# Low products at the seam of two up-projection pieces, and down steps gathered between the pairs

## The chip, the cores and the metric

The kernel runs on one core of one Trainium2 chip. The metric is the device time of one execution in microseconds (us). Five engines work side by side, each through its own list of instructions in order: TensorE multiplies matrices (in the profile PE, and PEld for its loads of stationary operands), VectorE (DVE) and ScalarE (ACT) do elementwise work, GpSimd (POOL) and SyncE (SP) here mostly start DMA transfers. An instruction that waits for a semaphore holds up everything behind it on its own engine.

## The reference

One layer of a hybrid encoder on a sequence of 256 tokens with model width 2048. The part that matters here is the convolutional feed-forward block at its end; the mixer ahead of it uses one changed helper as well.

```
x  = x + hybrid_mixer(rms_norm(x, attn_norm), ...)      # two kinds of attention, 16 heads
h  = rms_norm(x, ffn_norm)
u  = h @ w_up                                           # 2048 -> 2 * 5632, float32
u  = causal depthwise conv of width 3 over u, + conv_b  # per feature
gate, val = split(u)
x  = x + (silu(gate) * val) @ w_down                    # 5632 -> 2048
```

All inputs and outputs are float32.

## The kernel before, in words

**Precision.** TensorE is fed with the rounded type fp32r. Every operand is therefore kept as two parts, a high part (the value rounded to fp32r) and a low part (what the rounding lost), and a product is made as high x high + high x low + low x high. A weight tile of 128 x 2048 numbers (1 MB) arrives by a DMA in `w_raw`; ACT copies it to `w_hi` (line 202), then DVE computes `w_lo = w_raw - w_hi` (line 203). This pair is called the split of a tile. In the feed-forward block there are three buffers each for `w_hi` and `w_lo` and four for `w_raw`.

**Up steps.** The 11264 columns of `w_up` are made 256 at a time. Such a result is called a pair here, because it is made in two pieces: piece a takes the first 1024 of the 2048 rows, piece b the rest, both into the same two PSUM banks `pu` (`from_features`, line 244). A piece has 16 products with `w_hi`, each with 512 moving columns (activation high and low parts side by side; called wide), and 16 products with `w_lo` with 256 moving columns (high part alone; called narrow). Before the change both pieces do the wide ones first and then the narrow ones. The same helper makes queries and keys of the second kind of heads in the mixer, by way of `feature_major` (line 263), with two buffers for `w_hi` and two for `w_lo` there.

**Down steps.** The feed-forward width of 44 blocks of 128 features is cut into six parts: five of 8 blocks and a last one of 4. A part of 8 blocks is multiplied with its rows of `w_down` by a scheme that saves one of eight block products (`down_in_seven`, line 946): 7 steps for each half of the 2048 output columns, so 14 steps, called s1 to s14 here (s8 to s14 are the second half). Each has 12 wide products into one PSUM bank and afterwards one DVE addition of this bank into `x` (`added`, line 941). The banks of s1 to s7 are a, b, c, a, a, b, a; s8 to s14 repeat this with new tiles. The weights of s2, s4 and s7 (and s9, s11, s14) are three successive contents of one tile `w_sum`: DVE forms it from two loaded tiles (line 994), s2 splits it, then GpSimd starts a DMA that adds a third tile onto it in memory (`plus`, line 964), s4 splits the new content, another such DMA adds onto it, and s7 splits that. Beside the first of these DMAs a second one adds onto the loaded tile that s5 (s12) will use. The `w_sum` pool has one buffer.

**The order of the work.** The down steps of a part run between the up steps of the next part. A string tells how: u is the next up piece, s the next down step; `ORDER` serves the first five parts (the first has no down steps to do), `LAST_ORDER` the last, where the digits stand for the plain down product of the last part itself. The up pairs of a part are called P1 to P8 here: gate, value, gate, value and so on.

The loop at line 1094 writes all engines' instructions in this order by hand. In its pass n it issues, in this order: the load of step n+6; one advance of all follow-up work; the split of step n+2 (and the adding DMAs that hang on it); a second advance; the sum at line 994 for step n+4; and the products of step n. Follow-up work is a generator per step, advanced twice in a pass: for a down step the addition into `x` comes in the pass after it, ahead of that pass's split. For a pair it begins in the pass after piece b: ACT copies half of the PSUM result (842) and DVE adds and scales (843, 845) behind that pass's split; ACT makes the convolution taps (852, 859) a pass later; DVE sums them (864, and 879 for a value) ahead of the split in the third pass, and for values an ACT copy and DVE work (882, 884, and in some pairs 896 to 899, 906, 911) follow in the fourth and fifth.

In the mixer the instructions are ordered by a planner instead.

Of the kernel before, what the change touches and what calls it, by code (L numbers as in the profile page):

```python
# [14 lines left out]
P = 128  # L15
D = 2048
S = 256
NT = S // P
KT = D // P
# [18 lines left out]
FFN_PARTS = [(f, min(f + 8, NFT)) for f in range(0, NFT, 8)]  # L38


ORDER = "uuusususususususususususususus"
LAST_ORDER = "uususususususussss0s1ss3s2"


@with_exitstack
def hybrid_layer(
# [19 lines left out]
    nc = tc.nc  # L66
# [65 lines left out]
    hT = big.tile([P, KT, 2, S], F32R, name="hT")  # L132
# [99 lines left out]
    def token_major(lhs, w, k0, nk, c0, cols):  # L232

        acc = psa.tile([P, NT, 512], F32, name="acc", tag="acc")
        for k in range(0, nk, 4):
            parts = weights(rows_of(w, k0 + k, 4, c0, cols), 4, cols)
            in_three(
                [acc[:, t, :cols] for t in range(NT)], parts, 4,
                lambda i, part, t: of_half(lhs(k + i), part, t), k == 0, k + 4 == nk,
            )  # L240
            step()
        return acc

    def from_features(acc, parts, kh, n=8):

        hi, lo = parts
        for i0 in range(0, 8, n):
            for i in range(i0, i0 + n):
                k = 8 * kh + i
                for j in range(2):  # L250
                    nc.tensor.matmul(  # L251
                        acc[:, j, :], hi[:, i, j * P : (j + 1) * P],
                        hT[:, k].rearrange("p a b -> p (a b)"), start=k == 0, stop=False,
                    )
            for i in range(i0, i0 + n):
                k = 8 * kh + i
                for j in range(2):
                    nc.tensor.matmul(  # L258
                        acc[:, j, S:], lo[:, i, j * P : (j + 1) * P], hT[:, k, 0, :],
                        start=False, stop=k == KT - 1,  # L260
                    )

    def feature_major(w, c0, pool, tag):

        acc = pool.tile([P, 2, 512], F32, name="pu", tag=tag)
        for kh in range(2):
            from_features(acc, weights(rows_of(w, 8 * kh, 8, c0, 2 * P), 8, 2 * P), kh)
            step()
        return acc
# [9 lines left out]
    with ExitStack() as actx:  # L279
# [9 lines left out]
        def project(c0, cols):  # L289
            return token_major(lambda k: hT[:, k], wi, 0, KT, c0, cols)  # L290
# [198 lines left out]
        low = big.tile([P, 2, 16 * P], F32R, name="low", tag="x2")  # L489
# [41 lines left out]
        for j in range(3):  # L531
            acc = project(2 * WF + 344 * j, 344)
            n = 344 if j < 2 else 336
# [212 lines left out]
        for half in range(2):  # L746
# [6 lines left out]
            acc = project(B0 + 2 * WF + 512 * half, 512)  # L753
# [16 lines left out]
        for group in range(2):  # L770
# [3 lines left out]
            for c in range(4):  # L774
                acc = token_major(lambda k: oT[group * NH + k], wo, group * NH, NH, 512 * c, 512)
# [6 lines left out]
                if c == 0:  # L782
                    pg = psb.tile([P, NT], F32, name="pg", tag="t")
                    for t in range(NT):
                        nc.tensor.matmul(
                            pg[:, t : t + 1], ssq[group][:, t * P : (t + 1) * P], ones[:, 0:1],
                            start=t == 0, stop=t == NT - 1,
# [125 lines left out]
    def up_pieces(part, f0, follows):  # L913

        c0 = f0 * P + (DFF if follows is val_follows else 0)
        cell = []

        def piece(kh):
            mem = {}

            def loads():
                mem["raw"] = load(rows_of(wu, 8 * kh, 8, c0, 2 * P))

            def prepare():
                mem["parts"] = split(mem["raw"], 8, 2 * P)

            def matmuls():
                if kh == 0:
                    cell.append(psa.tile([P, 2, 512], F32, name="pu", tag="acc"))
                from_features(cell[0], mem["parts"], kh, 8 if c0 else 4)  # L930

            new_step(loads, None, prepare, matmuls, (lambda: follows(part, cell[0], f0)) if kh else None)

        piece(0)
        yield
        piece(1)
        yield
# [76 lines left out]
    def down_plain(part, c):  # L1014

        n = (part.f_hi - part.f_lo) // 4

        ends = LAST_ORDER[-1] == str(c // 512)
        sizes = [(0, 0, 512), (1, 0, 256), (1, 256, 256)] if ends else [(t, 0, 512) for t in range(NT)]
# [45 lines left out]
    for f_lo, f_hi in FFN_PARTS:  # L1065
# [9 lines left out]
        if f_hi == NFT:  # L1075
            steps_of |= {str(i): [down_plain(part, 512 * i)] for i in range(4)}
        for g in ORDER if f_hi < NFT else LAST_ORDER:
            if steps_of[g]:
# [81 lines left out]
```

## Time and profile before

| what | value |
|---|---|
| median of 3 runs | 1105.21 us (1105.05 to 1105.63) |
| the profiled execution's own time | 1106.53 us |
| its span, first to last instruction | 1104.8 us |
| granted TensorE clock over the span | 1.00 |
| busy share of the span | PE 99%, PEld 86%, DVE 79%, ACT 64%, POOL 4% |
| up pieces (32 products each) | 104: 88 in the feed-forward block, 16 in the mixer |
| down steps of 12 products | 70 |

The times of the profile are in microseconds from the first instruction. A row of the timeline gives start, duration, engine, line, operation, tiles written and read with their shapes, and how many instructions were merged; brackets give idle time ahead of it and what ended that. Matmuls overlap, so the length of a run of products is read from its start to the start of the next run, not from its duration.

### The profile page before, as it was taken

The numbers are of one execution on the slowest core, as the hardware profiler recorded it, in microseconds if no ns is written. First come the engines' busy times: TensorE is split into PE (matmuls) and PEld (weight loads), VectorE is DVE, ScalarE is ACT, GpSimd is POOL, SyncE is SP. The second block draws the span as 40 slices with busy tenths as digits, with TensorE's granted clock in tenths as the row PEclk, the third lists the DMA queues.
The fourth block names the chain that finished last, engine by engine and source line by source line (L and its number), as shares of the span: only waits on it lengthen the run. The fifth ranks groups of instructions, "written<-read, shape, count | busy, mean of one in ns | idle before, by whom it ended". The sixth has DMA issues, their size and how long they took to land. (4 is left out here: it accounts for less than half of the span.)

```text
span 1104.8 us, 14832 instructions
## 1 busy us (share of the span) xinstructions
PE 1098.9 (99%) x5872; PEld 951.9 (86%) x5872; DVE 875.6 (79%) x940; ACT 701.9 (64%) x879; POOL 44.4 (4%) x46
## 2 busy tenths in 40 slices
PE   9999999999999999999999999999999999999998
PEld 7998888888888888888888888888888888888887
DVE  5755777677775677679889988889798889889896
ACT  6544555556653567667767776767676677667753
POOL 0000000000000000000000010100000010100010
PEclk9999999999999999999999999999999999999999
DMA  8776555557555395558989597986979688987985
GB/s 290 183 230 229 189 156 156 187 153 247 173 161 184 113 313 196 194 181 204 292 222 311 190 235 263 263 268 177 317 208 308 210 222 273 253 266 192 325 212 161
DMA packets 179407, 245.96 MB, mean 223 GB/s; under 512 B 4432, under 2 KB 119018, under 8 KB 179082
## 3 DMA queue, kind: packets, MB, share of 16 engines
q1 hardware_dynamic: 162458, 209.73, 58.2%
q0 software_dynamic: 16560, 34.75, 16.7%
q8 instruction: 46, 0.75, 0.3%
q10 hardware_dynamic: 320, 0.53, 0.1%
q14 instruction: 23, 0.19, 0.0%
HBM read 242.89 MB, written 2.11 MB: 222 GB/s over the span
## 5 line engine op out<-in xcount | busy, mean ns | idle before, releaser
L203 DVE TENSOR_TENSOR w_lo<-w_raw,w_hi 128x2048 fp32r<-128x2048 f32 (+1 forms) x196 | 439.7, 2246 | 148.4 <-ACT w_hi L202 147.7
L202 ACT CAST w_hi<-w_raw 128x2048 fp32r<-128x2048 f32 (+1 forms) x196 | 367.1, 1876 | 255.6 <-PE pu L251 77.8
L251 PE MATMUL pu<-hT,w_hi 128*128 128x512 f32 x1664 | 397.0, 390 | 0.0
L251 PEld LDWEIGHTS pu<-hT,w_hi 128*128 128x128 f32 x1664 | 309.4, 188 | 62.4
L258 PEld LDWEIGHTS pu<-hT,w_lo 128*128 128x128 f32 x1664 | 213.6, 191 | 8.2
L258 PE MATMUL pu<-hT,w_lo 128*128 128x256 f32 x1664 | 216.5, 283 | 0.0
L224 PE MATMUL acc<-w_hi,hT 128*128 128x512 f32 (+1 forms) x576 | 125.8, 369 | 0.0
L224 PEld LDWEIGHTS acc<-w_hi,hT 128*128 128x128 f32 x576 | 101.3, 188 | 14.1
L202 ACT CAST w_hi<-w_sum 128x2048 fp32r<-128x2048 f32 x30 | 57.3, 1910 | 43.3 <-PE pu L251 36.5
L203 DVE TENSOR_TENSOR w_lo<-w_sum,w_hi 128x2048 fp32r<-128x2048 f32 x30 | 68.7, 2289 | 19.9 <-ACT w_hi L202 19.8
L859 ACT ACTIVATE tap<-up,ccol 128x256 f32<-128x256 f32 x176 | 74.6, 495 | 0.0
L224 PE MATMUL acc<-w_lo,hT 128*128 128x512 f32 (+1 forms) x288 | 64.6, 366 | 0.0
L224 PEld LDWEIGHTS acc<-w_lo,hT 128*128 128x128 f32 x288 | 51.6, 188 | 7.5
L964 POOL DMA_DIRECT2D w_sum<-in_w_down_dram x20 | 25.7, 1285 | 769.8 <-DVE w_lo L203 758.5
L224 PE MATMUL acc<-w_hi,oT 128*128 128x512 f32 x192 | 46.2, 393 | 0.0
L224 PEld LDWEIGHTS acc<-w_hi,oT 128*128 128x128 f32 x192 | 35.6, 188 | 7.3
L224 PE MATMUL bank_a<-w_hi,s 128*128 128x512 f32 x160 | 40.1, 393 | 0.8 <-ACT w_hi L202 0.8
L224 PE MATMUL bank_a<-w_hi,g 128*128 128x512 f32 x160 | 40.0, 392 | 0.0
L224 PE MATMUL bank_b<-w_hi,s 128*128 128x512 f32 x160 | 40.0, 392 | 0.0
L224 PEld LDWEIGHTS bank_a<-w_hi,s 128*128 128x128 f32 x160 | 28.8, 189 | 6.4 <-ACT w_hi L202 1.2
L224 PEld LDWEIGHTS bank_a<-w_hi,g 128*128 128x128 f32 x160 | 28.9, 189 | 5.2
L224 PEld LDWEIGHTS bank_b<-w_hi,s 128*128 128x128 f32 x160 | 28.9, 189 | 5.3
(214 smaller groups left out, 1072.3 us busy)
## 6 DMA issues: line engine op xcount, KB each, us to landing
w_raw<-in_w_up_dram SPq DMA_DIRECT2D x88, 1024.0 KB, 7.6
w_raw<-in_w_down_dram SPq DMA_DIRECT2D x44, 1024.0 KB, 6.4
w_raw<-in_w_in_dram SPq DMA_DIRECT2D x36, 1024.0 KB, 5.2
w_sum<-in_w_down_dram POOLq DMA_DIRECT2D x20, 1024.0 KB, 10.1
w_raw<-in_w_out_dram SPq DMA_DIRECT2D x16, 1024.0 KB, 5.1
w_raw<-in_w_down_dram POOLq DMA_DIRECT2D x10, 1024.0 KB, 14.8
w_raw<-in_w_in_dram SPq DMA_DIRECT2D x12, 688.0 KB, 4.2
w_raw<-in_w_in_dram SPq DMA_DIRECT2D x6, 512.0 KB, 6.7
```

The lines of the kernel that those rows point to most:

```text
L202: act.copy(hi[:, :n], raw[:, :n])
L203: dve.tensor_tensor(lo[:, :n], raw[:, :n], f32(hi[:, :n]), op=ALU.subtract)
L224: nc.tensor.matmul(o, lhs(i, l, t), r[:, i, :], start=starts and j == 0, stop=stops and j == 3 * n - 1, skip_group_check=more,)
L251: nc.tensor.matmul(acc[:, j, :], hi[:, i, j * P : (j + 1) * P], hT[:, k].rearrange("p a b -> p (a b)"), start=k == 0, stop=False,)
L258: nc.tensor.matmul(acc[:, j, S:], lo[:, i, j * P : (j + 1) * P], hT[:, k, 0, :], start=False, stop=k == KT - 1,)
L859: act.activation(taps[w][:, j, :], u[:, j, w : w + S], AF.Copy, scale=ccol[:, w, f : f + 1])
L964: nc.gpsimd.dma_start(mem[into][:, : nk * 512].rearrange("p (a b) -> p a b", a=nk), src, accum_op=ALU.add)
```

## The change

Two things are edited. In `from_features` piece b (`kh` = 1) does its narrow products first and its wide ones after them, while piece a keeps wide then narrow. And the two order strings put the two pieces of a pair one right after the other, with two or three down steps between pairs. Written out, a middle part goes

before: `u u u s1 u s2 u s3 u ... s13 u s14`

after: `P1a P1b P2a P2b s1 s2 P3a P3b s3 s4 P4a P4b s5 s6 P5a P5b s7 s8 P6a P6b s9 s10 s11 P7a P7b s12 s13 P8a P8b s14`

and the last part begins `P1a P1b s1 P2a P2b s2 s3 s4 P3a P3b s5 s6 P4a P4b s7 s8 s9 s10 0 s11 1 s12 s13 3 s14 2`; from s7 on this is as before, where the letters ahead of s7 were `u u s1 u s2 u s3 u s4 u s5 u s6 u`. The numbers of products, splits, loads and additions stay the same, and so do all buffers and the distances 6, 4 and 2 of the loop.

```diff
-ORDER = "uuusususususususususususususus"
-LAST_ORDER = "uususususususussss0s1ss3s2"
+ORDER = "uuuu" + "ssuu" * 4 + "sssuu" + "ssuu" + "s"
+LAST_ORDER = "uusuusssuussuussss0s1ss3s2"
@@ def from_features(acc, parts, kh, n=8):
         hi, lo = parts
+
+        def high(k, i, j):
+            nc.tensor.matmul(
+                acc[:, j, :], hi[:, i, j * P : (j + 1) * P],
+                hT[:, k].rearrange("p a b -> p (a b)"), start=k == 0, stop=k == KT - 1,
+            )
+
+        def low(k, i, j):
+            nc.tensor.matmul(
+                acc[:, j, S:], lo[:, i, j * P : (j + 1) * P], hT[:, k, 0, :], start=False, stop=False,
+            )
+
         for i0 in range(0, 8, n):
-            for i in range(i0, i0 + n):
...
-            for i in range(i0, i0 + n):
...
+            for product in (low, high) if kh else (high, low):
+                for i in range(i0, i0 + n):
+                    for j in range(2):
+                        product(8 * kh + i, i, j)
```

More of the change, by code (lines that the diff above doesn't have):

```diff
@@ L246, in from_features @@
         hi, lo = parts
-        for i0 in range(0, 8, n):
-            for i in range(i0, i0 + n):
[L249 to L254, printed above, removed]
-            for i in range(i0, i0 + n):
[L256 to L261, printed above, removed]
+        def high(k, i, j):
[7 more added lines that the diff above has]
+            )
+        for i0 in range(0, 8, n):
+            for product in (low, high) if kh else (high, low):
+                for i in range(i0, i0 + n):
+                    for j in range(2):
+                        product(8 * kh + i, i, j)
     def feature_major(w, c0, pool, tag):
```

## Prediction

> **What bounds the kernel now.** I read the page's head first, then the busy time of one whole middle part, then the timeline of TensorE.
>
> ```profile
> span 1104.8 us, 14832 instructions
> PE 1098.9 (99%) x5872; PEld 951.9 (86%) x5872; DVE 875.6 (79%) x940; ACT 701.9 (64%) x879; POOL 44.4 (4%) x46
> core 0: us, PE busy (x) PEld busy (x) DVE busy (x) ACT busy (x) POOL busy (x), PEclk, DMA share, GB/s
> 746.97:874.12 127.15, 127.15 (x683) 110.26 (x682) 111.77 (x99) 89.57 (x99) 7.78 (x6) 1.00 0.88 248
> ```
>
> TensorE has no pause in a middle part (127.15 of 127.15 us), at full clock. DVE follows at 111.77, 88%. So the change can gain only where a product itself becomes shorter, and loses wherever TensorE is made to wait. Four stretches of TensorE (between stretches the rows are not adjacent):
>
> ```profile
> 425.88 3.82 PE L251 MATMUL pu<-hT,w_hi 128*128 128x512 f32 x16
> 429.53 0.64 PE L258 MATMUL pu<-hT,w_lo 128*128 128x256 f32 x4
> ...
> 688.96 2.00 PE L224 MATMUL bank_a<-w_hi,g 128*128 128x512 f32 x8
> 690.80 1.07 PE L224 MATMUL bank_a<-w_lo,g 128*128 128x512 f32 x4
> 691.71 3.79 PE L251 MATMUL pu<-hT,w_hi 128*128 128x512 f32 x16
> 695.34 2.08 PE L258 MATMUL pu<-hT,w_lo 128*128 128x256 f32 x16
> 697.25 2.00 PE L224 MATMUL bank_b<-w_hi,s 128*128 128x512 f32 x8
> ...
> 1059.30 1.98 PE L224 MATMUL bank_a<-w_hi,g 128*128 128x512 f32 x8
> 1061.11 1.07 PE L224 MATMUL bank_a<-w_lo,g 128*128 128x512 f32 x4
> ```
>
> From start to start: an up piece is 697.25 - 691.71 = 5.54 us (wide 3.63, narrow 1.91); a down step is 1.81 + .91 = 2.72. A wide run is longer behind a narrow one: 3.65 against 3.63 in an up piece (425.88 comes behind narrow products, 691.71 behind wide ones), and 690.80 - 688.96 = 1.84 against 1.81 in a down step. That is .02 to .03 us for each passage from narrow to wide.
>
> **The change part by part.**
>
> *Narrow products at the seam.* Each of the 104 pieces now ends in such a passage; afterwards each of the 52 pairs has one. 52 x .02 to .03 = 1.0 to 1.6 us are saved. Of a narrow run behind a narrow one no row exists; I set .01 each against it, .5. I take -1.0 us (ends -1.6 and 0).
>
> *When buffers come free and what is due.* The split of step n+2 writes the buffers of step n-1. ACT begins about .25 us after the last wide product of that step (687.29 behind 687.05 in the next fence). After a piece b this is now its end, 1.91 us later than before. And piece b needs `w_lo` at its first product, 3.63 us earlier than before. To see what this costs I lay out the queue of DVE; its pace is in these rows.
>
> ```profile
> 683.31 2.28 DVE L994 TENSOR_TENSOR w_sum<-w_raw 128x2048 f32<-128x2048 f32 x1
> 685.51 0.68 DVE L884 TENSOR_TENSOR g<-gate,g 128x512 fp32r<-128x512 f32 x1
> 686.11 0.68 DVE L941 TENSOR_TENSOR x<-x,bank_a 128x512 f32<-128x512 f32 x1
> 686.71 2.28 DVE L203 TENSOR_TENSOR w_lo<-w_raw,w_hi 128x2048 fp32r<-128x2048 f32 x1
> 687.05 2.08 PE L258 MATMUL pu<-hT,w_lo 128*128 128x256 f32 x16
> 687.29 1.91 ACT L202 CAST w_hi<-w_sum 128x2048 fp32r<-128x2048 f32 x1 [2.61 <-PE pu L251]
> 689.24 2.29 DVE L203 TENSOR_TENSOR w_lo<-w_sum,w_hi 128x2048 fp32r<-128x2048 f32 x1 [0.25 <-ACT w_hi L202]
> 691.45 0.68 DVE L843 TENSOR_TENSOR t<-pu,t 128x512 f32<-128x512 f32 x1
> 691.82 1.28 POOL L964 DMA_DIRECT2D w_sum<-in_w_down_dram  x1 [40.00 <-DVE w_lo L203]
> 692.17 0.69 DVE L845 TENSOR_TENSOR up<-t,R 128x512 f32<-128x512 f32 x1
> 692.77 0.68 DVE L941 TENSOR_TENSOR x<-x,bank_a 128x512 f32<-128x512 f32 x1
> 695.57 1.48 DVE L864 TENSOR_TENSOR gate<-gate,tap 128x512 f32<-128x512 f32 x2
> 703.82 1.91 ACT L202 CAST w_hi<-w_sum 128x2048 fp32r<-128x2048 f32 x1 [2.62 <-PE pu L251]
> ...
> DMA to landing us min/median/max: 8.2/10.1/14.4
> w_sum<-in_w_down_dram POOLq DMA_DIRECT2D x1, 1024.0 KB, 8.2
> w_sum<-in_w_down_dram POOLq DMA_DIRECT2D x1, 1024.0 KB, 8.6
> w_sum<-in_w_down_dram POOLq DMA_DIRECT2D x1, 1024.0 KB, 12.5
> ```
>
> Back to back, a line 203 or 994 takes 2.20 us of the queue, a line 941 .60, lines 843 and 845 .72 and .60, two of line 864 1.40 (.6 more with line 879). The adding DMA starts .29 us after the low split of s9 (691.82 against 689.24 + 2.29) and lands after 8.2 (this one), 8.6 (the same place a part later) or, where it starts while another addition and loads are under way, 12.5. In the order before, from the split of s9 (687.29) to that of s11 (703.82) there are four steps, 16.5 us, and the DMA is over 3.8 us ahead (691.82 + 8.2 = 700.0).
>
> *s9, s10, s11 in a row.* Now s9 is split in the pass of P6a and s11 in the pass of s9: two up pieces apart, 11.1 us, while low split, start and landing alone take 1.9 + 2.3 + .3 + 8.4 = 12.9. Let Z be the start of s7; TensorE without pauses would then start s8 at 2.72, P6a 5.44, P6b 10.98, s9 16.52, s10 19.24, s11 21.96, P7a 24.68, P7b 30.22. DVE, in program order: the low split of P6a waits for ACT (.25 + 1.91: the buffer is P5b's) and starts at 2.16; 843 and 845 of P5 at 4.36 and 5.08; the sum 994 for s9 at 5.68 (its pass is that of s7); the addition of s7 at 7.88; low split of P6b 8.48; addition of s8 10.68; 864 twice for P5 11.28; low split of s9 12.68 to 14.97. The DMA starts at 15.26, lands at 23.66 (8.4, the mean of the two places of its kind), ACT splits s11 by 25.6: a pause of 3.7 us at s11. Its low part is ready at 27.9 where the wide products end at 27.5, .5 more; P7a starts at 28.9 instead of 24.68.
>
> ACT stood still meanwhile, and DVE behind it. From the low split of s11 (25.7) it does 843 and 845 of P6 27.9, the addition of s9 29.2, low split of P7a 29.8 to 32.1 (due at 28.9 + 3.63, in time), addition of s10 32.0, 864 and 879 of P6 32.6, low split of P7b 34.6 to 36.9. P7b begins with narrow products, and would start at 34.4: a second pause of 2.5 us. With the wide ones first nothing would wait. Together 36.9 - 30.2 = 6.7 us in each of the four middle parts with down steps: **26.8 us**. With a landing of 8.2 or 10.1 us and .5 us either way in the queue this is 6.0 to 8.9 a part.
>
> *s2, s3, s4 in the last part.* The same form: s2 is split in the pass of P2a, s4 in that of s2, two up pieces apart, with the previous part's last pair on DVE in place of the sum. I take **6.7** again, between 0 and 8.9.
>
> *Other piece b's.* By the same count the low split of P6b ends at 10.8 and is due at 10.98: just in time, up to .5 a part more if the queue is slower. Elsewhere two down steps and an up piece (11 us) lie between, no cost.
>
> *The tail.* From s7 of the last part the order is as before, but the buffer for s9 is that of a piece b and comes free 1.91 us later. In the rows below, everything that hangs on it is late already:
>
> ```profile
> 1068.37 1.91 ACT L202 CAST w_hi<-w_sum 128x2048 fp32r<-128x2048 f32 x1 [2.36 <-DMA w_sum<-in_w_down_dram]
> 1076.43 5.53 ACT L202 CAST w_hi<-w_raw 128x2048 fp32r<-128x2048 f32 x3 [4.34 <-DMA w_raw<-in_w_down_dram]
> 1078.38 2.29 DVE L203 TENSOR_TENSOR w_lo<-w_raw,w_hi 128x2048 fp32r<-128x2048 f32 x1 [2.37 <-ACT w_hi L202]
> 1081.19 0.68 DVE L941 TENSOR_TENSOR x<-x,bank_a 128x512 f32<-128x512 f32 x1
> 1082.01 2.09 PE L224 MATMUL bank_a<-w_hi,s 128*128 128x512 f32 x8 [0.79 <-ACT w_hi L202]
> ```
>
> ACT waits for the landing before s12's split, DVE for ACT, the addition of s11 stands behind it, and s12 writes the same bank: it starts right after that addition. I add the full shift, **1.9** (0 to 1.9).
>
> *Down steps in twos.* No two neighbours share a bank, so an addition into `x` holds nobody up: no cost. Loads by SP come at the same distance in steps. A raw tile is late at times already:
>
> ```profile
> ACT w_hi L202 <- DMA w_raw<-in_w_up_dram: 30.0, 14, 4.6
> ```
>
> (total, times, longest), and TensorE in its middle parts never paused for it: 0, up to 3.
>
> *In the mixer* the 8 pieces b need their low part earlier, and 8 splits start 1.9 us later:
>
> ```profile
> 236.30 1.91 ACT L202 CAST w_hi<-w_raw 128x2048 fp32r<-128x2048 f32 x1 [1.34 <-PE pu L251]
> 238.24 2.29 DVE L203 TENSOR_TENSOR w_lo<-w_raw,w_hi 128x2048 fp32r<-128x2048 f32 x1 [2.68 <-ACT w_hi L202]
> 244.70 0.63 PE L251 MATMUL pu<-hT,w_hi 128*128 128x512 f32 x2
> ```
>
> The low split ends at 240.5, then at 242.4, and the piece starts at 244.70: covered by 2.3 us. The heads' work queued behind shifts too: 0, up to 1 us for each, 8.
>
> Sum: -1.0 + 26.8 + 6.7 + 1.9 = +34.4 us. Against the profiled execution's span this is 1104.8 + 34.4 = 1139.2; its own time, 1106.53, stands 1.3 above the median, so I add to the median: 1105.21 + 34.4 = **1139.6 us**.
>
> **The rivals.**
>
> A. *The landing is hidden; not slower.* If the low split of s9 were done 4 us earlier, by 11 after Z, s11 would not wait, and P7b neither: 1105.2 - 1.0 + (0 to 1.9) = 1104 to 1106. For it: DVE is only 88% busy. Against: the queue above is full from 2.2 to 15, and no landing was under 8.2.
>
> B. *Only the first pause.* If DVE catches up during it (843 to 879 of P6 run earlier than I place them), P7b does not wait: 5 x 4.2 + 1.9 - 1.0 = +21.9, 1127. Against: these operations need the copy at line 842, which is behind the blocked split on ACT.
>
> C. *The addition lands as late as 12.5 us*, as it did beside other transfers. 4.1 us more in each of five places: 1160. For it: loads for P7 and s10 are in flight in that window. Against: they were in the 8.2 and 8.6 too. [...]
>
> D. *The gain is larger.* Were a passage worth over twice my rows, 1102.
>
> **How the numbers follow.** Forecast .68, A .12, B .12, C .06, D .02. The range must hold the forecast with its bounds (five places of 6.0 to 8.9, up to 8 from the mixer) and B: 1122 to 1158. A measurement of this kernel can tell about .2%, 2.2 us, from no change. Faster: .03 (D and a little of A). Same: .10 (A). Slower: .87.
>
> **What would show it.** Five pauses of about 4 us on TensorE ahead of a `w_hi` of `w_sum` whose ACT copy waited for the adding DMA, each followed 9 us later by one of 2 to 3 us in which narrow products wait for line 203; s12 in the tail about 2 us later against s11; wide runs in up pieces of 3.63 throughout. The prediction is wrong if ACT never waits at those copies, or if the pauses are there and P7b starts without one.

## The result, and the profile after

The changed kernel takes 1147.24 us (median, 1145.66 to 1148.54) against 1105.22 us (1104.88 to 1105.63): 1.0378 times as long, 95% interval 1.0367 to 1.0388, or 42.0 us more. The forecast was 1139.6 (1122 to 1158). The profiled execution took 1148.54 us, its span is 1146.8, 42.0 over that of before. From line 262 on, line numbers are two higher than before (943 for 941, 966 for 964), and the wide and narrow products of an up piece stand in lines 249 and 255.

The head of the page after:

```profile
span 1146.8 us, 14823 instructions
PE 1112.0 (97%) x5872; PEld 959.4 (84%) x5872; DVE 874.5 (76%) x940; ACT 693.0 (60%) x879; POOL 44.4 (4%) x46
```

Two stretches of about one middle part each; they begin and end 3 to 5 us ahead of an s7 (time, then busy time of each engine with its instructions, granted clock, DMA share, GB/s):

```profile
559.11:692.61 133.50, 129.25 (x676) 111.32 (x675) 110.25 (x98) 86.69 (x98) 7.71 (x6) 0.97 0.84 235
692.61:826.65 134.04, 128.34 (x676) 110.56 (x675) 110.16 (x99) 86.54 (x99) 7.77 (x6) 0.99 0.84 233
```

From s7 to the next s7 (562.10, 696.60 and 831.46) it is 134.50 and 134.86 us. Such a part took 127.15 us, all of it busy, at clock 1.00; now TensorE stands still for 4.25 and 5.70 us of the two stretches, and their mean clock is .97 and .99.

One pause in the timeline, in the first part with down steps. Z, the start of s7, is 562.10 here:

```profile
570.63 2.29 DVE L203 TENSOR_TENSOR w_lo<-w_raw,w_hi 128x2048 fp32r<-128x2048 f32 x1
574.83 2.29 DVE L203 TENSOR_TENSOR w_lo<-w_sum,w_hi 128x2048 fp32r<-128x2048 f32 x1
577.41 1.27 POOL L966 DMA_DIRECT2D w_sum<-in_w_down_dram  x1 [44.90 <-DVE w_lo L203]
578.16 1.83 POOL L966 DMA_DIRECT2D w_raw<-in_w_down_dram  x1
586.44 1.90 ACT L202 CAST w_hi<-w_sum 128x2048 fp32r<-128x2048 f32 x1 [9.67 <-DMA w_sum<-in_w_down_dram]
588.38 2.29 DVE L203 TENSOR_TENSOR w_lo<-w_sum,w_hi 128x2048 fp32r<-128x2048 f32 x1 [9.06 <-ACT w_hi L202]
588.39 3.78 PE L224 MATMUL bank_a<-w_hi,s 128*128 128x512 f32 x8 [4.14 <-ACT w_hi L202]
593.68 4.07 PE L249 MATMUL pu<-hT,w_hi 128*128 128x512 f32 x16
597.43 2.28 DVE L203 TENSOR_TENSOR w_lo<-w_raw,w_hi 128x2048 fp32r<-128x2048 f32 x1
599.77 1.97 PEld L255 LDWEIGHTS pu<-hT,w_lo 128*128 128x128 f32 x16 [0.31 <-DVE w_lo L203]
```

The adding DMA starts behind the low split of s9, lands 9.0 us later, ACT has waited 9.67 us for it, TensorE starts s11 at 588.39, and DVE has stood still for 9.06 us. At 597.43 comes the low split of P7b.

The chains of waits of the whole run (total, times, longest):

```profile
ACT w_hi L202 <- DMA w_sum<-in_w_down_dram: 53.2, 7, 10.5
PE bank_a L224 <- ACT w_hi L202: 22.5, 6, 5.0
PE pu L255 <- DVE w_lo L203: 3.9, 4, 1.2
```

To see every loss I took the distance from each matmul's start to the next one's and subtracted the regular spacing (.2267 us for 512 columns, .120 for 256). Summed by region, in us:

| kernel | first 30 us | to the end of the mixer | part 1 (ups alone) | parts 2 | 3 | 4 | 5 | last part and tail |
|---|---|---|---|---|---|---|---|---|
| before | 3.79 | 3.56 | .48 | .35 | .32 | .32 | .32 | 1.23 |
| after | 5.14 | 5.48 | .32 | 7.67 | 8.03 | 8.50 | 7.88 | 9.34 |

The differences add up to 42.0: parts 2 to 5 +30.8, last part and tail +8.1, mixer +1.9, part 1 -.2, and +1.35 in the first 30 us, where nothing was changed: this execution ran at clock .50 from 7.1 to 10.5 us, the one of before at 1.00. The kernels below, which start alike, lost 3.1 to 3.6 there.

The mixer's two pauses, where the heads' work comes later, and the two in the tail:

```profile
253.45 0.52 PE L597 MATMUL ps_p<-cs,e 128*128 128x128 f32 x3 [0.93 <-DVE e L739]
280.06 0.52 PE L597 MATMUL ps_p<-cs,e 128*128 128x128 f32 x3 [0.67 <-DVE e L739]
...
1111.43 1.66 PE L1039 MATMUL acc<-w_hi,g 128*128 128x512 f32 x6 [0.84 <-DVE g L886]
1124.02 2.08 PE L224 MATMUL bank_a<-w_hi,s 128*128 128x512 f32 x8 [0.96 <-ACT w_hi L202]
```

### The profile page after: what moved, and what is told of

It is laid out like the page before. It is cut to its first block, busy times and chain, and to the rows that moved or that the text cites. A ratio compares the mean times of both kernels' runs of the same rounds, so it can differ in the third digit from the quotient of the medians.

```text
span 1146.8 us, 14823 instructions
## 1 busy us (share of the span) xinstructions
PE 1112.0 (97%) x5872; PEld 959.4 (84%) x5872; DVE 874.5 (76%) x940; ACT 693.0 (60%) x879; POOL 44.4 (4%) x46
## 5 line engine op out<-in xcount | busy, mean ns | idle before, releaser
L255 PEld LDWEIGHTS pu<-hT,w_lo 128*128 128x128 f32 x1664 | 207.5, 191 | 9.2 <-DVE w_lo L203 5.0
L255 PE MATMUL pu<-hT,w_lo 128*128 128x256 f32 x1664 | 211.3, 283 | 4.0 <-DVE w_lo L203 3.9
L224 PE MATMUL bank_a<-w_hi,s 128*128 128x512 f32 x160 | 46.6, 440 | 22.5 <-ACT w_hi L202 22.5
L224 PEld LDWEIGHTS bank_a<-w_hi,s 128*128 128x128 f32 x160 | 33.3, 212 | 32.1 <-ACT w_hi L202 25.0
L854 ACT ACTIVATE gate<-up,ccol 128x256 f32<-128x256 f32 x44 | 24.1, 595 | 23.3 <-DVE up L847 15.0
L854 ACT ACTIVATE val<-up,ccol 128x256 f32<-128x256 f32 x44 | 24.1, 595 | 23.0 <-DVE up L847 22.8
## 6 DMA issues: line engine op xcount, KB each, us to landing
w_raw<-in_w_down_dram POOLq DMA_DIRECT2D x10, 1024.0 KB, 15.4
```

Of the source, the lines that this page charges most:

```text
L224: nc.tensor.matmul(o, lhs(i, l, t), r[:, i, :], start=starts and j == 0, stop=stops and j == 3 * n - 1, skip_group_check=more,)
L255: nc.tensor.matmul(acc[:, j, S:], lo[:, i, j * P : (j + 1) * P], hT[:, k, 0, :], start=False, stop=False,)
L854: act.activation(a[:, j, :], u[:, j, 2:], AF.Identity, scale=ccol[:, 2, f : f + 1], bias=ccol[:, 3, f : f + 1],)
```

## The experiments

Four of the kernels undo or keep one part of the change; the others look for where an order of pairs could go without the pause, which tests the prediction's other terms: buffers, banks, loads and landings. "Lost" is TensorE's lost time by the table's measure in parts 2, 3, 4, 5 and the last.

**The orders alone**: the two strings of the change, with `from_features` as it was (wide products first in every piece).

```diff
-            for product in (low, high) if kh else (high, low):
-                for i in range(i0, i0 + n):
-                    for j in range(2):
-                        product(8 * kh + i, i, j)
+            for i in range(i0, i0 + n):
...
+            for i in range(i0, i0 + n):
...
```

> The changed order strings alone; every up piece keeps wide products first. [...] Forecast 1105.2 + 5 x 3.3 = 1121.7 us (1117 to 1127). Rival (narrow products first are the cause, by taking buffers late and wanting the low part early): without them no pause is left and the time is 1105 to 1107 us.

Measured: 1126.75 us, 1.0186 times before (1.0163 to 1.0210). Lost: 4.05, 5.34, 5.12, 4.52, 4.24. From the timeline, a pause of the first part and the products behind it, and (windows) the granted clock behind the same pause a part later:

```profile
583.02 2.14 PE L224 MATMUL bank_a<-w_hi,s 128*128 128x512 f32 x8 [2.54 <-ACT w_hi L202]
585.35 1.21 PE L224 MATMUL bank_a<-w_lo,s 128*128 128x512 f32 x4 [0.19 <-DVE w_lo L203]
586.40 3.82 PE L251 MATMUL pu<-hT,w_hi 128*128 128x512 f32 x16
```

```profile
711.30:714.70 3.40, 0.28 (x2) 0.26 (x2) 0.28 (x1) 2.21 (x2) 0.00 (x0) 0.99 1.10 261
714.70:718.10 3.40, 3.40 (x9) 2.62 (x9) 3.37 (x4) 2.00 (x3) 1.09 (x1) 0.50 1.11 243
```

Five pauses ahead of s11 and s4 (2.71, 3.28, 2.93, 2.71, 1.78 us), the five places of the forecast, and none at P7b. No run shows its 3.3 us for a place; lost were 4.05 to 5.34. The forecast has no half clock in it, and behind three of the pauses there is one: the 3.4 us from 714.70, behind 3.28, ran at .50. So the orders by themselves bring half of the loss, and the order of the products lengthens each pause by the later buffer: 2.71 became 4.30 in the first part with down steps, 1.6 us, with a buffer that comes free 1.91 us later. The landings differ too (9.3, 9.9, 9.6, 9.3 and 8.4 us here, 9.0, 9.3, 9.8, 9.2 and 8.3 in the changed kernel); with that difference taken out, each of the five pauses grew by 1.95 to 1.99 us.

**The order of the products alone** (order strings as before):

```diff
-ORDER = "uuuu" + "ssuu" * 4 + "sssuu" + "ssuu" + "s"
-LAST_ORDER = "uusuusssuussuussss0s1ss3s2"
+ORDER = "uuusususususususususususususus"
+LAST_ORDER = "uususususususussss0s1ss3s2"
```

> Narrow products first in every piece b, with the order strings of before. Theory: between the splits of s9 and s11 there are four steps again, so no pause over 3 us in the feed-forward middle parts; what is left is the mixer (about 1.7 us), the tail (1.3 to 1.9 us) and no gain from the seams, since the pieces of a pair do not touch. Forecast 1108.5 us (1106 to 1111). Rival (narrow-first makes DVE late for piece b): 44 pairs wait for the low split, 0.5 us or more each, 1125 us or more.

Measured: 1112.82 us, 1.0058 (1.0039 to 1.0077): more than expected. Lost: .62, 1.44, .80, .62, 4.18, and 5.14 up to the end of the mixer against 3.56. Its chains of waits:

```profile
PE bank_a L224 <- DVE x L943: 2.2, 3, 1.1
PE pu L255 <- DVE w_lo L203: 1.2, 1, 1.2
```

The pauses are short and at different places: 1.18 and .85 us in the mixer, 1.03 and .40 in parts 3 and 4, 1.36, 1.0 and 1.3 in the last part and the tail. An adding DMA onto `w_sum` is behind none of them. (The 1.3 at s12 in the tail hangs on the second adding DMA, onto s12's own tile, as its .95 did before the change.) Alone, the two edits cost 21 and 7 us; together 42, since the pause at s11 takes both delays and P7b then waits as well.

**The changed kernel without the first adding DMA onto `w_sum`** (the addition is left out of the result; the second one, which goes out with it, stays):

```diff
-            sums=first_sum, then=lambda: (plus("w", w22), plus("12", w22)),
+            sums=first_sum, then=lambda: plus("12", w22),
```

> The changed kernel without the first adding DMA onto w_sum (that of the third weight tile ahead of s4 and s11; this part of the sum of weights is left out, the other addition beside it and the later one stay). Theory: the split of s11 has nothing to wait for, all five long pauses and the short ones behind them go, the granted clock is back at 1.00: 1105.2 - 1.0 + 1.7 (mixer) + 1.3 to 1.9 (tail) + up to 2.5 (low split of P6b just in time) = 1108 us (1106 to 1111). Rival (the packed order makes DVE or ACT late whether or not the DMA is there): pauses ahead of s11 or P7b stay, over 1120 us.

Measured: 1107.15 us, 1.0009 (1.0000 to 1.0019). Lost: .16, .16, .16, .16, 1.40. The group of the page that holds s11's products, here and in the changed kernel:

```profile
L224 PE MATMUL bank_a<-w_hi,s 128*128 128x512 f32 x160 | 39.5, 389 | 0.0
```

```profile
L224 PE MATMUL bank_a<-w_hi,s 128*128 128x512 f32 x160 | 46.6, 440 | 22.5 <-ACT w_hi L202 22.5
```

All five pauses are gone, the second ones at P7b and the half clock with them (mean clock 1.00 against .988): some 40 us hang on this addition. This kernel also moves ten transfers of 1 MB less, so by itself it does not part the landing from the load on the DMA engines; that it is the landing is read from the changed kernel, where ACT's wait of 9.67 us ends with it. What stays is the mixer and 1.0 in the tail. In parts 2 to 5 it loses .16 where the kernel before lost .32: that is the seam's gain, .16 for 8 pairs.

**Narrow products first in the mixer alone:**

```diff
-ORDER = "uuuu" + "ssuu" * 4 + "sssuu" + "ssuu" + "s"
-LAST_ORDER = "uusuusssuussuussss0s1ss3s2"
+ORDER = "uuusususususususususususususus"
+LAST_ORDER = "uususususususussss0s1ss3s2"
...
-            for product in (low, high) if kh else (high, low):
+            for product in (low, high) if kh and narrow else (high, low):
...
-            from_features(acc, weights(rows_of(w, 8 * kh, 8, c0, 2 * P), 8, 2 * P), kh)
+            from_features(acc, weights(rows_of(w, 8 * kh, 8, c0, 2 * P), 8, 2 * P), kh, 8, True)
```

> Narrow-first in piece b of the mixer's eight pairs alone; the feed-forward block as before the change. In the profile of the changed kernel the mixer lost 1.8 us more than before in two pauses ahead of a head's transposes. Forecast 1107.2 us (1106.4 to 1108.2). Rival (these pauses come from elsewhere): 1105.4 us.

Measured: 1109.22 us, 1.0030 (1.0018 to 1.0043), 3.0 us above the runs of before beside it. The profile shows the same two pauses ahead of `ps_p` (1.18 and .84 us), 1.65 more lost in the mixer, and a span 1.3 longer. The other 1.4 to 1.7 us of the median do not show in the profiled execution. The five longest of its ten executions (1110.0 to 1113.0 us) have a mean granted clock of .997 or .998, the other five of .999 or 1.00, so stretches of half clock are a likely part of it; what sets them off here stays open.

**Three steps in a row at the end of a part**, so that s9 and s11 are again two up pieces and a down step apart:

```diff
-ORDER = "uuuu" + "ssuu" * 4 + "sssuu" + "ssuu" + "s"
-LAST_ORDER = "uusuusssuussuussss0s1ss3s2"
+ORDER = "uuuu" + "ssuu" * 5 + "suu" + "sss"
+LAST_ORDER = "uussuussuussuussss0s1ss3s2"
```

> The changed kernel with other groups of down steps: in the middle parts two after each pair from P2 to P6, s11 alone behind P7, s12 s13 s14 behind P8; in the last part s1 s2 behind P1, s3 s4 behind P2, s5 s6 behind P3. So the split of s11 stands four steps behind that of s9 (P6a, P6b, s9, s10), and that of s4 four behind that of s2; still no two neighbours in one bank. Theory: the pauses go, while narrow-first, pairs and seams stay: 1105.2 - 1.0 + 1.7 + 1.3 to 1.9 = 1107.5 us (1105 to 1111), clock 1.00. Rival (down steps in groups of two and three starve TensorE of splits): pauses at the groups stay, 1120 us or more.

Measured: 1118.88 us, 1.0117 (1.0096 to 1.0137). Lost: 1.33, 1.34, 1.65, 2.39, 7.22. From its chains of waits:

```profile
PE bank_a L224 <- DVE x L943: 5.4, 5, 1.3
PE pu L255 <- DVE w_lo L203: 2.6, 2, 2.1
```

No pause at s11, as expected. Missed was the bank: s12 and s14 write bank a with one step between, and the addition of s12 is not through DVE in those 2.7 us: 1.07 to 1.42 us in each part. The last part lost most, 6 us more than before: P3a waits 1.5 us and P3b 2.3, for two up tiles landed 14.9 and 16.4 us after their issue, beside the two adding DMAs.

**Three steps at s7 to s9, the last part as before, wide products first everywhere**, and **the same with narrow products first in piece b of the first five parts:**

```diff
-ORDER = "uuuu" + "ssuu" * 4 + "sssuu" + "ssuu" + "s"
-LAST_ORDER = "uusuusssuussuussss0s1ss3s2"
+ORDER = "uuuu" + "ssuu" * 3 + "sssuu" + "ssuu" * 2 + "s"
+LAST_ORDER = "uususususususussss0s1ss3s2"
```

and for the second of them also

```diff
-            for product in (low, high) if kh else (high, low):
+            for product in (low, high) if kh and narrow else (high, low):
...
-                from_features(cell[0], mem["parts"], kh, 8 if c0 else 4)
+                from_features(cell[0], mem["parts"], kh, 8 if c0 else 4, part.f_hi < NFT)
```

> The same order strings as in the run before (group of three s7 s8 s9, last part as before the change), but every piece with wide products first. Theory: no pause and no passage saved, so as the kernel before, 1105.4 us (1104.9 to 1106.5); the difference to the run before is the worth of the seams alone, .8 us. Rival (groups of down steps cost by themselves): 1108 us or more.

> The idea of the change with the causes found so far taken out: in the first five parts piece b has its narrow products first and pairs stay together, but the group of three is s7 s8 s9, with s10 s11, s12 s13 and s14 behind P6, P7 and P8, so that from the split of s9 to that of s11 lie s7, s8, s9 and P6a, 13.7 us, and another 8.3 us from there to the products of s11; the last part has the order and the product order of before, and the mixer the product order of before. Theory: no pause is left, 40 passages from narrow to wide at .02 us are saved: 1104.7 us (1104.0 to 1105.8), against 1105.4 for the kernel before. Rival (any narrow-first piece makes DVE late somewhere): 1108 us or more.

Measured: 1109.44 us, 1.0024 (1.0014 to 1.0035), with the wide ones first; 1121.57 us, 1.0141 (1.0121 to 1.0160), with the narrow ones first. Lost: .35, .78, 2.57, .32, 1.23, and 2.10, 7.70, 2.74, 6.70, 2.24. The largest pause of the second, from its timeline:

```profile
709.54 1.91 ACT L202 CAST w_hi<-w_raw 128x2048 fp32r<-128x2048 f32 x1 [7.18 <-DMA w_raw<-in_w_up_dram]
717.85 1.90 ACT L202 CAST w_hi<-w_raw 128x2048 fp32r<-128x2048 f32 x1 [5.92 <-DMA w_raw<-in_w_up_dram]
719.78 2.29 DVE L203 TENSOR_TENSOR w_lo<-w_raw,w_hi 128x2048 fp32r<-128x2048 f32 x1 [4.08 <-ACT w_hi L202]
722.13 3.14 PE L255 MATMUL pu<-hT,w_lo 128*128 128x256 f32 x13 [4.61 <-DVE w_lo L203]
```

and the worst place of the first:

```profile
844.07 3.92 PE L251 MATMUL pu<-hT,w_hi 128*128 128x512 f32 x16 [0.31 <-ACT w_hi L202]
855.85 1.20 PE L224 MATMUL bank_b<-w_lo,s 128*128 128x512 f32 x4 [1.38 <-DVE w_lo L203]
```

Both misses have one cause, which I had set at nothing: the raw tiles of P7a and P7b arrive late. ACT waits 63.1 and 66.6 us in all for such tiles, against 30.0 before. With the wide products first a late tile of piece b has 3.63 us more, for the narrow ones need the low part last, and it costs .3 us at once and 1.4 us twelve us later, since DVE, which had waited 3.9 us for that tile, is still behind; with the narrow ones first the low split (2.29) stands between landing and start, and TensorE waits 4.61 us. In the changed kernel ACT waits 17.9 us for such loads; the likely reason is that the pause at s11 gives them time.

**Two steps at a time throughout**, so that s11 and s12 stand side by side and share bank a (otherwise as the narrow-first kernel just shown):

```diff
-ORDER = "uuuu" + "ssuu" * 3 + "sssuu" + "ssuu" * 2 + "s"
+ORDER = "uuuu" + "ssuu" * 6 + "ss"
```

> As the kernel with the group s7 s8 s9 and narrow-first in the first five parts, but with plain groups of two: s9 s10 behind P6, s11 s12 behind P7, s13 s14 behind P8. s11 and s12 write one bank, so s12 must wait until DVE has added s11's result into x. That addition is issued in s12's own pass, takes .7 us and can find DVE busy with a low split: a pause of 1 to 2 us in each of four parts, 1104.7 + 6 = 1110.7 us (1107 to 1114). Rival (DVE adds in the shadow of the next products): 1104.7 us as the run with the group of three.

Measured: 1136.89 us, 1.0268 (1.0250 to 1.0285). Lost: 7.84, 5.68, 6.58, 6.50, 8.18. Its chain of waits, and the first such pause in the timeline:

```profile
PE bank_a L224 <- DVE x L943: 19.3, 5, 5.3
```

```profile
590.89 3.71 ACT L202 CAST w_hi<-w_raw 128x2048 fp32r<-128x2048 f32 x2 [4.84 <-DMA w_raw<-in_w_down_dram]
592.84 4.49 DVE L203 TENSOR_TENSOR w_lo<-w_raw,w_hi 128x2048 fp32r<-128x2048 f32 x2 [2.33 <-ACT w_hi L202]
598.57 0.68 DVE L943 TENSOR_TENSOR x<-x,bank_a 128x512 f32<-128x512 f32 x1
599.40 2.90 PE L224 MATMUL bank_a<-w_hi,s 128*128 128x512 f32 x6 [5.26 <-DVE x L943]
```

I had counted the addition and a part of one low split, 1 to 2 us. It comes behind two low splits and the work on P7 in DVE's queue, and the first of these splits, that of s12, waited (2.33 us, by way of ACT) for the second adding DMA, which adds onto s12's own tile and landed 16.6 us after its issue (574.21 to 590.8). ACT waits 4.84, 3.25, 3.33 and 4.05 us for it in the four middle parts. So the pauses of 3.8 to 5.4 us are not the bank's alone: the order also puts s12 too near the addition that it needs, and the shared bank hands that delay on. What the bank would cost without it was not run.

**The narrow-first order of pairs with less on the DMA engines**: the second adding DMA left out (of the result too).

```diff
-            sums=first_sum, then=lambda: (plus("w", w22), plus("12", w22)),
+            sums=first_sum, then=lambda: plus("w", w22),
```

> The order of seams, without the addition onto the loaded tile that s12 uses (the second of the two adding DMAs that go out together, 1 MB; it is left out of the result too). In seams the pauses (1.86, 4.77, 1.91, 4.00 us) stood ahead of P7b, whose raw tile landed late. Theory, the transfers share the DMA engines: between the start of that addition and the landing of P7b's tile they were full (share 1.1 at 275 to 291 GB/s), so 1 MB less brings the tile 1.05 / .283 = 3.7 us earlier: pauses of about 0, 1.1, 0, .3, and with the half clock behind them gone 1107.5 us (1105 to 1111). Rival, the tile is late because its buffer comes free late, or because DVE and ACT get to its split late: the pauses stay, 1119 us or more.

Measured: 1104.01 us, .9979 (.9970 to .9988). Lost: .16, .16, .16, .16, .15. Its chains of waits:

```profile
ACT w_hi L202 <- DMA w_sum<-in_w_down_dram: 6.8, 5, 2.4
ACT w_hi L202 <- DMA w_raw<-in_w_up_dram: 1.7, 2, 1.0
```

The wait for loads goes from 66.6 to 1.7 us, and no pause is left. So the lateness hangs on this addition, and the forecast by the mean rate (3.7 us earlier) was too small. About 1 us of the time is no gain of the order: in the tail s12 has no addition to wait for any more, and the pause of .95 us that the kernel before has there is gone. The queue that carries the additions takes more of the DMA engines' time here than its bytes alone account for. The two queues of the narrow-first kernel with all its additions (packets, MB, share of the time of 16 engines):

```profile
q1 hardware_dynamic: 162458, 209.73, 57.6%
q0 software_dynamic: 16560, 34.75, 16.5%
```

A MB of the second queue, where the additions are most of the bytes (30 of 1.05 MB each), takes .47% of the span, one of the first .27%.

**Three steps at s5 to s7** (otherwise as the narrow-first kernel):

```diff
-ORDER = "uuuu" + "ssuu" * 3 + "sssuu" + "ssuu" * 2 + "s"
+ORDER = "uuuu" + "ssuu" * 2 + "sssuu" + "ssuu" * 3 + "s"
```

> As seams (narrow products first in piece b of the first five parts alone, last part in the order of before), with the three down steps at s5, s6, s7 instead of s7, s8, s9: between the start of the two adding DMAs behind the split of s9 and the need for P7b's tile lie an up piece instead of a down step more, 5.5 us against 2.7. Theory, crowded DMA engines make that tile late: the pauses of seams shrink by 2.8 us to about 0, 1.9, 0, 1.2, with little half clock: 1107.5 us (1105 to 1112). Rival, the lateness is carried along from the rotation of the four raw buffers, not from the distance: pauses as in seams, 1117 to 1122. Second rival, s5 to s7 in a row make a pause of their own at s7 (its split needs the addition that starts behind s4): s4 and s7 are as far apart as s2 and s4 were in a pair plus one step, so none is expected.

Measured: 1114.87 us, 1.0081 (1.0067 to 1.0095). Lost: 1.35, 3.94, 3.61, 1.33, 2.76.

```profile
PE pu L255 <- DVE w_lo L203: 4.3, 2, 2.3
PE bank_a L224 <- DVE x L943: 3.6, 4, 0.9
```

The pauses at P7b shrank from 1.86, 4.77, 1.91, 4.00 to 0, 2.50, 0, 2.16, near the expected 0, 1.9, 0, 1.2: distance from the additions counts. The rest is the bank again: s5 and s7 share bank a with s6 between, 1.07 us in each part. I had looked at the landing ahead of s7 and not at its bank.

**The second addition issued two passes earlier**, right behind the sum at line 996, in the narrow-first kernel with three steps at s7 to s9, and in the changed kernel:

```diff
             dve.tensor_tensor(w, x, y, op=ALU.add)
+            plus("12", w22)
...
-            sums=first_sum, then=lambda: (plus("w", w22), plus("12", w22)),
+            sums=first_sum, then=lambda: plus("w", w22),
```

> The order and products of seams, all the work done; the second adding DMA (onto the tile that s5 and s12 use) is issued right behind the sum at line 996, two passes earlier, and no longer beside the adding DMA onto w_sum. Theory, crowded DMA engines: in seams they were busy .70 in the 14 us ahead of the two additions and over 1.0 in the 22 us behind, so 1 MB fits ahead; the pauses ahead of P7b go as they went in seams_light, and the time is 1104.4 us (1103.6 to 1107), by the seam's gain under the kernel before. Rival, it is the sum of all transfers that is too much: P7b's tile stays late, 1113 us or more.

> The changed kernel with the second adding DMA issued right behind the sum at line 996. If its transfer beside the first is what made the landings 9.0 to 9.8 us instead of the 8.2 and 8.6 of before, they come down to 8.2 to 8.6, each of the five pauses by about .9 us, and the time is 1142.7 us (1139 to 1145). Rival, the landings are set by loads or by the addition itself: they stay at 9 to 9.8 and the time at 1146 to 1149. Under both the wait for the landing stays, and with it over 30 us.

Measured: 1107.67 us, 1.0017 (1.0008 to 1.0026), and 1167.88 us, 1.0550 (1.0534 to 1.0566). The first lost .16, .16, .16, .16, 4.28: TensorE waits for no late load in any part of 8 blocks, with all the work done, but the last part lost 3 us more than before. The second lost 11.23, 12.05, 13.48, 11.40, 15.07, 20.6 us more than the changed kernel. Last part of the first, and the first pause of the second:

```profile
1051.96 1.28 POOL L966 DMA_DIRECT2D w_raw<-in_w_down_dram  x1 [23.52 <-DVE w_sum L996]
1057.66 1.28 POOL L966 DMA_DIRECT2D w_sum<-in_w_down_dram  x1 [4.42 <-DVE w_lo L203]
1071.76 1.90 ACT L202 CAST w_hi<-w_sum 128x2048 fp32r<-128x2048 f32 x1 [7.49 <-DMA w_sum<-in_w_down_dram]
1073.71 1.65 PE L224 MATMUL bank_a<-w_hi,s 128*128 128x512 f32 x3 [2.40 <-ACT w_hi L202]
```

```profile
568.73 1.27 POOL L966 DMA_DIRECT2D w_raw<-in_w_down_dram  x1 [38.15 <-ACT tap L861]
575.49 1.28 POOL L966 DMA_DIRECT2D w_sum<-in_w_down_dram  x1 [5.49 <-DVE w_lo L203]
588.08 1.90 ACT L202 CAST w_hi<-w_sum 128x2048 fp32r<-128x2048 f32 x1 [13.22 <-DMA w_sum<-in_w_down_dram]
```

Where the other addition is under way when the one onto `w_sum` starts (568.73 to its landing at 580.5), the latter takes 12.5 us in place of 9.0, and TensorE pauses 7.86 us. At s2 of the next part of the same kernel the other one has landed .3 us before (649.2), and the one onto `w_sum` takes 8.75. In the changed kernel the two go out .75 us apart and the first one issued lands first: 9.0 us against 15.5 for the other. Both theories of the second run fall: the landing was neither shortened by the early issue nor independent of it. Of two under way together the first issued landed first in these runs, and the changed kernel already has the right one in front.

No version here that does all the work is faster than the kernel before by more than can be told. With the last part's additions as they were, the first of these two would lose there between 1.23 us (the kernel before) and 2.24 (the narrow-first kernel) in place of 4.28, so 1104.6 to 1105.6 us; that is an estimate, and was not run.

## Why the prediction was right, and where its sizes were off

The sum was +34.4 and +42.0 was measured; sign, places and mechanism were those forecast, and the removal of one adding DMA takes the loss away.

- *Seam, -1.0.* Right: the first part, where nothing else changes, went from .48 to .32, .02 for each pair; 52 pairs make 1.04.
- *First pauses, 3.7 each.* Their place and cause are right: DVE's queue came out almost to the step (adding DMA at Z + 15.31, forecast 15.26), P6b had its low part just in time and lost nothing. The term that was too small is the landing: 9.0, 9.3, 9.8, 9.2 in the middle parts against 8.4, and so pauses of 4.30, 4.66, 5.16, 4.52 (and 3.69 in the last part, with 8.3). The order of the products is not what makes them longer than the rows of before at the same place (8.2 and 8.6): with it alone the four are 8.5 to 8.6, with the orders alone 9.3 to 9.9. What in the orders does it no run here isolates; 10.1, the upper bound I used, held.
- *Second pauses at P7b, 2.5 each.* They are .3, 1.35, .56, 1.36 and 1.25, so the sign "the pauses are there and P7b starts without one" was all but met in the first part. Yet P7b starts as late as forecast, and later by the longer landing: at Z + 37.7 (599.77), 38.0, 38.5 and 37.9 in the four middle parts against Z + 36.9, and .6, .9, 1.4 and .8 us of that are the landing. DVE sets it, as the layout of its queue said: from 588.38 to the end of P7b's low split at 599.71 it works without a pause. What I had not foreseen fills the time between. Behind each of the four pauses the granted clock fell to .50, for 6.83, 3.41, 6.83 and 3.41 us, and s11 and P7a ran so slowly (s11 5.29 us in the first of these parts, 2.72 at full clock) that less waiting was left. In these parts the half clock therefore costs nothing of its own; it takes time in which TensorE would have waited for DVE. From the windows of the changed kernel:

```profile
580.00:587.40 7.40, 4.26 (x19) 3.19 (x17) 0.00 (x0) 0.96 (x1) 0.00 (x0) 1.00 1.09 228
587.40:594.20 6.80, 5.80 (x14) 4.56 (x15) 5.79 (x5) 5.39 (x8) 1.27 (x1) 0.50 1.11 233
594.20:600.00 5.80, 5.69 (x34) 4.86 (x33) 5.66 (x7) 5.38 (x6) 0.00 (x0) 1.00 1.08 237
```

  Rival B (first pause alone, 1127) falls with P7b's start and with the table: the loss of a part was 7.3 to 8.2 over before, not 4.2. Forecast 6.7, bounds 6.0 to 8.9.
- *Last part, 6.7.* About 6.9 of the 8.1 of last part and tail; *tail, 1.9*: about 1.2, and not where I put it. At s12 TensorE stands still 1.12 us where it stood .95 before, .2 more, for there the landing of the second adding DMA sets the time and not the buffer that comes free 1.9 us later; 1.0 is new ahead of the last part's own product (line 1039, waiting for `g`), which I had not looked at, and that pause is there also in the kernel without the first adding DMA.
- *Mixer, 0.* Missed: +1.9, from two pauses of the heads (1.18 and .84 us), and 1.65 in the kernel that changes the mixer alone. I compared the low split with its piece (2.3 us of cover, which held) and set the heads' work behind it to 0 with a bound of 1 us each.
- *Loads, 0.* Right in the sum and wrong in its reason. Loads at the same distance in steps are not on time by that: in the pairs' order without a pause at s11 they are late and cost 15 us.
- *Rival A* (landing hidden) falls with the 9.67 us of ACT's wait. *Rival C*, 12.5 us, did not occur here, but such a landing is real: with another addition issued ahead of it, the same one took 12.5 to 14.8 us in the middle parts and the kernel 1167.9. The row of 12.5 that I took it from I had read wrongly, though: that addition starts at 708.38, and the other one (692.58, 15.0 us to landing) had landed .8 us before. Two loads of SP start beside it (713.67 and 718.06); what stretched it no run here isolates.

The sizes together: the later P7b +4.6 over the forecast for four parts (3.7 of it the longer landing), mixer +1.9, start +1.35, last part and tail -.4, make 7.45 of the 7.6 us missing; the rest is rounding in these terms.

## What to carry to other kernels

In a schedule written by hand, a step has several kinds of slack at once (the distance from a producing DMA, from the last user of its buffer and of its bank, from its load), and regrouping the steps spends all of them; here every regrouping that restored one ran into the next. Before a gain of .02 us per place is bought by such a move, lay out the queue of the engine with the least room in program order, as done here for DVE, and take the landing of a transfer from a moment with as much beside it as there will be afterwards (onto `w_sum` 12.5 us beside the other addition, 8.75 with that one landed). And a cost that reads zero beside a pause must be looked at again once that pause is gone.

## What was not expected of the hardware

- The granted clock fell to .50 behind pauses for 3.41 or 6.83 us, and was back at 1.00 after that. In the changed kernel it did so behind all five first pauses: 6.83 us behind 4.30 and 5.16, 3.41 us behind 4.66, 4.52 and 3.69. At its start 3.41 us at .50 (from 7.10) follow a pause of 1.46 that ended at 6.79. The second pauses at P7b (.3 to 1.36 us) had no half clock behind them. In the kernel with the orders alone it came behind pauses of 3.28, 2.93 and 2.71 us, while another of 2.71 and one of 1.78 had none, and with three steps at s5 to s7 pauses of 2.50 and 2.16 left the mean clock of the execution at 1.00. So the length of a pause alone does not part the cases; what does, no run here isolates.
- Two adding DMAs issued .75 us apart landed 9.0 and 15.5 us after their issue (.74 to .90 apart, 8.3 to 9.8 and 15.4 to 15.8 us, at the five places of the changed kernel), and the one onto `w_sum` took 12.5 when the other had been issued 6.8 us ahead of it.
- In the narrow-first order of pairs, leaving out one 1 MB addition per half part, 10 of some 246 MB, took the wait for loads from 66.6 to 1.7 us.
